# Two PSUM places for the branch products, joined transposes, a final norm in halves, and ten more gates computed early

## The chip, the cores and the metric

The kernel runs on one core of a Trainium2 chip. A core has five engines that work from queues of their own: PE (matrix products), DVE and POOL (elementwise work), ACT (functions and copies) and SP (here only the issuing of transfers). The metric is the device time of one execution in microseconds (us); for the kernel before, three runs gave 1998.32, 1999.73 and 2000.26, median 1999.73.

## The reference

Two layers, each a pre-norm residual layer with three token mixers side by side, on 512 tokens of 1024 channels, all in float32:

```python
def hybrid_layer(x, ...):
    h = rms_norm(x, norm_w)
    p = h @ w_in                        # 1024 x 13440
    xa, ga, pb, pc, pm = jnp.split(p, [OFF_GA, OFF_B, OFF_C, OFF_M], axis=-1)
    y_a = rglru_branch(xa, ...) * silu(ga)     # convolution, gates, scan over tokens
    y_b = rwkv7_branch(pb, ...)                # 16 heads of 64, a state per head updated token by token
    y_c = retention_branch(pc)                 # 4 heads of 256, causal scores with decay
    proj = jnp.einsum("nbsw,nwd->bsnd", ys, w_branch)   # 3 x (1024 x 1024)
    gates = sigmoid(pm + b_merge)              # 3 x 1024 gate channels
    merged = sum over branches of gates * proj
    return x + merged @ w_out
# after two layers: rms_norm(x, final_norm_w)
```

## The kernel before

Everything is kept transposed: channels on the 128 partitions, the 512 tokens along the free axis. A projection (`proj`, line 566) turns one 128-channel block of weights into one 128x512 result: the weight block is loaded (`raw`), split into a rounded part and a remainder (`whi` by ACT, `wlo` by DVE; `weights`, line 557), and eight channel tiles of the input, split the same way, give 24 matmuls into one PSUM tile called `acc`. A layer has 129 such projections: inputs of the three mixers, 24 merge gates (`gate`, line 1109), 24 branch products (`branch`, line 1123: eight for each of the branches b0, b1, b2) and eight output products.

The mixer of the RWKV branch works on two 128-channel blocks at a time, a "head group" (four per layer). For each it has a preparation (`p`), scores (`s`), a chain of eight steps over the token chunks (`c`, `rwkv_chain`) and an output part (`o`). In a chain step PE works three times for a moment (tile `p`), and in between ACT and DVE copy its results (`zs`, `sv`). The scores hold an inversion on POOL (`ex`, `etmp`, 62 operations). Three kinds of small products, `vt`, `w` (its second half) and `yt`, are written in the code once for each of the two blocks of the group.

Nothing is issued in the order of the code. A planner (`Scheduler`, line 156) records every operation, gives each tile slot out in the order of the program, and lists the operations by a cost table and due times; the engines' queues then hold that order, and each engine works through its own. The order of the program comes from the list `ORDER` (line 68): `l` is a part of the recurrent branch, `r` one of the retention branch, `g2` computes the four gates 8 to 11 early and stores them in DRAM (`gsc`), `b0 b2 b1` are the branches at the end of a layer. A gate that was not stored is computed in `branch` right ahead of its product. In PSUM the projections have three places called "a" and one called "d"; a branch product always takes "d", and the next branch product can start once DVE has read it (`stt`, tile `thm`, and for b0 tile `mg`). Slots of SBUF tiles are given by `caps` (line 376): `raw` is a weight block as it was loaded.

All transfers go through SP's queue in order. The final norm (`sum_sq`, `rms_scale` and a loop at the end) sums the squares of the eight tiles `xr`, and multiplies each by its gain and by `rs` on DVE (two of the eight on POOL).

The matrix products of the small kind (`p`, `vt`, `w`, `yt`, `sc`, `lora`) use parts of the array ("tiled"), the projections all of it.

All engine instructions are recorded by one line, 368, so the profile's rows are told apart by the names of tiles: `yh`, `yq` and `ylo` are the inputs of branch products, `mq` that of the output products, `xh` and `xl` those of the first projections of a layer, `hh` and `hl` those of all the others.

Of the kernel before, what the change touches and what calls it, by code (L numbers as in the profile page):

```python
# [13 lines left out]
ACTF = mybir.ActivationFunctionType  # L14
# [3 lines left out]
P = 128  # L18
# [48 lines left out]

ORDER = "p0 l1 s0 l0 g2 p1 c0 l2 o0 s1 p2 g1 l3 c1 r0 o1 s2 r1 p3 c2 r2 o2 s3 r3 c3 o3 b0 b2 b1".split()

# [303 lines left out]
def hybrid_kernel(ctx: ExitStack, tc: tile.TileContext, xT, wt, par, cst, outT):  # L373
    nc = tc.nc
    S = Scheduler(nc)
    caps = {"h": 16, "tp": 16, "tc": 7, "tm": 14, "q": 12, "sv": 1, "raw": 3, "whi": 2, "wlo": 2,
            "zs": 2, "sn": 2, "pc": 2, "ssq": 2, "vm": 2, "vv": 2}
# [187 lines left out]

    def proj(l, w, movs, bank="a", wts=None):
        hi, lo = wts or weights(l, w)
        ps = tl(bank, "acc")
        with S.prio(4):
            for k0 in range(0, KT, 2):  # L570
                with S.group():
                    for k in (k0, k0 + 1):
                        whi, wlo = hi[:, k * P:(k + 1) * P], lo[:, k * P:(k + 1) * P]
                        mh, ml = movs[k]
                        mm(ps[:], whi, mh, k == 0, False, T)
                        mm(ps[:], whi, ml, False, False, T)
                        mm(ps[:], wlo, mh, False, k == KT - 1, T)
        return ps


    def sum_sq(xs, last=None):
        acc = []
        for k in range(KT):
            sq = tl("tm", "sq")
            act(sq[:], xs[k], ACTF.Square)
            if k < 2 or k == KT - 1:
                acc.append(sq)
            else:
                tt(acc[k % 2][:], acc[k % 2][:], sq[:], ALU.add)
            if last:  # L590
                last(k)

# [270 lines left out]
    def rwkv_scores(l, prep, g):  # L863
# [83 lines left out]
        sv = tl("sv", "sv", [P, NCH, 2, 2, HK])  # L947
        for i in range(2):
            ps = tl("rp", "vt", [P, NCH, HK])
            with S.group():  # L950
                for c in range(NCH):
                    for q in range(2):
                        mm(ps[half(q), c, :], v[i][:, c * CH:(c + 1) * CH], blkc[:, half(1 - q)], True, True, HK,
                           tiled="t")
            for q in range(2):
                act(sv[half(q), :, i, 1 - q, :], ps[half(q)], ACTF.Copy)

# [31 lines left out]
        for q in range(2):  # L989
            rr = slice(HK * q + 32, HK * q + 64)  # L990
            act(xw[rr, :, 0:256], ps[rr].rearrange("p i c t -> p i (c t)"), ACTF.Copy)
        for i in range(2):
            ps = tl("rp", "w2", [P, NCH, 32])
            with S.group():
                for c in range(NCH):
                    for q in range(2):
                        mm(ps[half(q), c, :], xw[:, i, 32 * c:32 * c + HK],
                           XD[i][:, c, HK * q + 32:HK * q + 64], True, True, 32, tiled="t")
            for q in range(2):
                rr = slice(HK * q, HK * q + 32)  # L1000
                act(XD[i][rr, :, HK * q + 32:HK * q + 64], ps[rr], ACTF.Copy, scale=-1.0)
        for s_ in range(2):
# [54 lines left out]
    def rwkv_out(l, h, sco, g):  # L1057
# [12 lines left out]
        with S.prio(1):  # L1070
# [7 lines left out]
            act(ssq[:], ssq[:], ACTF.Exp, scale=-0.5)  # L1078
            for i, j in enumerate(js):
                yn = yns[i]  # L1080
                tt(yn, XD[i][:, :, 0:HK], ssq[:, i, :].unsqueeze(2).to_broadcast([P, NCH, HK]), ALU.mult)
                ps = tl("rp", "yt", [P, NCH, CH])
                with S.group():
                    for c in range(NCH):
                        for q in range(2):
                            mm(ps[half(q), c, :], sco[1][i][:, c, 0, :], ident[:, half(1 - q)], True, True, CH, tiled="t")
                y = bonus[i]
# [35 lines left out]
    def branch(l, h, mg, b, where, first, last, stored):  # L1123
        ys = load_y(l, b, where)
        ms = []
        for m in range(KT):
# [6 lines left out]
            if first:  # L1133
                mg.append(tl("tm", "mg"))
            ps = proj(l, W_BR + 8 * b + m, ys, "d")
            with S.prio(0.6):
# [17 lines left out]
    for l in range(DEPTH):  # L1154
        with S.prio(1):
            xw = gained(l, xs)
            ps = sum_sq(xs)
        qs = [tl("tm", "q") for _ in range(4)]
# [41 lines left out]
        def do(kind, n):  # L1200
# [12 lines left out]
            elif kind == "g":  # L1213
                ns = range(4 * n, 4 * n + 4)
                gates(l, h, ns)
# [5 lines left out]
        for x in ORDER:  # L1221
            do(x[0], int(x[1]))
        xs = []
        xq = []
        with S.prio(3):
            for k in range(0, KT, 2):
                t = tl("q", "xr", [P, 2, T])
                for i in range(2):
                    dma(t[:, i], xT[k + i] if l == 0 else xsc[k + i], TILE_B)
                    xs.append(t[:, i])  # L1230
        for m in range(KT):
            ps = proj(l, W_OUT + m, ms, "ad"[m % 2])
            with S.prio(1):
                tt(xs[m], xs[m], ps[:], ALU.add)
    with S.prio(0):
        gain = [pcol(0, "final_norm_w", k) for k in range(KT)]
        ps = sum_sq(xs, lambda k: k % 4 == 1 and act(xs[k], xs[k], ACTF.Identity, scale=gain[k]))
        rs = rms_scale(ps)
        for k in range(KT):
            if k % 4 == 1:  # L1240
                ptt(xs[k], xs[k], rs[:], ALU.mult)
            else:
                stt(xs[k], xs[k], gain[k], rs[:], ALU.mult, ALU.mult)
            dma(outT[k], xs[k], TILE_B)

# [78 lines left out]
```

## Time and profile before

| what | value |
|---|---|
| median of three runs | 1999.73 us |
| the profiled execution | 1998.77 us |
| its span, first to last instruction | 1996.9 us |
| PE busy | 1955.3 us |
| DVE, ACT, POOL busy | 1276.2, 893.7, 571.4 us |
| granted clock of PE, mean | 0.997 |
| transfers | 206.59 MB, mean 103 GB/s |
| weight blocks loaded | 281 of 512 KB, 3.3 us from issue to landing (median) |

The span is 1.87 us shorter than the execution's own time, and that execution is 0.96 us below the median of the runs. Matmuls are pipelined: each shows as busy for about 0.39 us, though the next one starts 0.227 us after it. A busy share of 98% therefore hides short delays, and starts of rows are the better measure. "Idle before" is time in which an engine did nothing ahead of an instruction, with the instruction that ended the wait.

### The profile page before, as it was taken

Reading aid. Unit: us, or ns where it says so; the run is one execution under the profiler, and the core shown is the slowest. Engines: PE = TensorE matmul, PEld = TensorE weight load, DVE = VectorE, ACT = ScalarE, POOL = GpSimd, SP = SyncE. Lnnn points to the kernel's source line nnn. Section 1 sums busy time; section 2 is a strip of 40 time slices with the busy share of each in tenths; the row PEclk is TensorE's granted clock in tenths of the full one; section 3 lists DMA queues with packets and bytes.
Section 4 is the critical chain, followed back from the end, with each engine's and each line's share of the span. In section 5 each row is a group of like instructions: output and inputs, shape, how many; then the busy total and the mean of one; then the engine's idle time right before and its main releaser. Section 6 shows DMA issues by size and latency. Waiting matters only on the chain.

```text
span 1996.9 us, 32028 instructions
## 1 busy us (share of the span) xinstructions
PE 1955.3 (98%) x12792; PEld 1537.1 (77%) x12792; DVE 1276.2 (64%) x1885; ACT 893.7 (45%) x1366; POOL 571.4 (29%) x790
## 2 busy tenths in 40 slices
PE   9999999999999999999999999999999999999997
PEld 6778778868877887778878787787788787768785
DVE  8995677678567753444569747785875687443534
ACT  7663735262344343432357546444432634342322
POOL 1137125521812361000012542273326125400000
PEclk9999999999999999999999999999999999999998
DMA  4243133322322343243522432332223123332441
GB/s 171 87 119 117 64 108 101 96 70 80 109 64 90 106 122 123 87 156 95 178 89 87 133 100 75 109 105 76 86 77 111 54 93 109 121 117 95 151 145 63
DMA packets 104069, 206.59 MB, mean 103 GB/s; under 512 B 42608, under 2 KB 43888, under 8 KB 103920
## 3 DMA queue, kind: packets, MB, share of 16 engines
q1 hardware_dynamic: 103920, 204.55, 31.7%
q8 instruction: 101, 1.65, 0.3%
q14 instruction: 48, 0.39, 0.1%
HBM read 179.34 MB, written 25.17 MB: 102 GB/s over the span
## 4 chain that ended last, share of the span: by engine, by line
PE 86%; DVE 6%; POOL 4%; issue 1%; DMA 1%; ACT 1%; DVEq 0%; SPq 0%; ACTq 0%; POOLq 0%
PE acc L368 65%; PE p L368 5%; PE vp L368 4%; POOL etmp L368 2%; PE rout L368 2%; POOL ex L368 2%; PE w L368 2%; PE sc L368 2%; PE rsc L368 2%; PE gate L368 1%; DVE wlo L368 1%; DVE bk L368 1%; PE yt L368 1%; PE kss L368 1%; PE vt L368 1%
## 5 line engine op out<-in xcount | busy, mean ns | idle before, releaser
L368 ACT ACTIVATE whi<-raw 128x1024 fp32r<-128x1024 f32 (+1 forms) x283 | 298.7, 1055 | 734.8 <-PE acc L368 587.4
L368 PE MATMUL acc<-hh,whi 128*128 128x512 f32 x1488 | 609.7, 410 | 0.1
L368 PE MATMUL acc<-hh,wlo 128*128 128x512 f32 x1488 | 582.4, 391 | 2.9 <-DVE wlo L368 2.9
L368 PE MATMUL acc<-hl,whi 128*128 128x512 f32 x1488 | 580.7, 390 | 0.0
L368 DVE TENSOR_TENSOR wlo<-raw,whi 128x1024 fp32r<-128x1024 f32 (+1 forms) x283 | 365.7, 1292 | 214.4 <-ACT whi L368 211.5
L368 PEld LDWEIGHTS acc<-hh,whi 128*128 128x128 f32 x1488 | 279.2, 188 | 70.8 <-issue 6.5
L368 PEld LDWEIGHTS acc<-hh,wlo 128*128 128x128 f32 x1488 | 279.3, 188 | 65.8 <-DVE wlo L368 5.8
L368 PEld LDWEIGHTS acc<-hl,whi 128*128 128x128 f32 x1488 | 279.8, 188 | 55.9 <-issue 3.8
L368 POOL TENSOR_TENSOR etmp<-ex,ea 64x31 f32<-64x31 f32 (+15 forms) x248 | 174.6, 704 | 44.9 <-DMA ea<-ead 26.2
L368 POOL TENSOR_TENSOR ex<-ex,etmp 64x31 f32<-64x31 f32 (+15 forms) x248 | 172.7, 696 | 19.2
L368 POOL TENSOR_TENSOR dec<-sv,pc 64x128 f32<-64x128 f32 x96 | 48.2, 503 | 403.6 <-DVE sv L368 400.2
L368 ACT ACT_TABLE_LOAD x87 | 111.6, 1283 | 2.3 <-PEq L1315 0.7
L368 PE MATMUL acc<-yh,whi 128*128 128x512 f32 x256 | 104.1, 407 | 8.2 <-DVE thm L368 5.0
L368 PE MATMUL acc<-yh,wlo 128*128 128x512 f32 x256 | 100.2, 391 | 0.0
L368 PE MATMUL acc<-ylo,whi 128*128 128x512 f32 x256 | 99.9, 390 | 0.0
L368 POOL TENSOR_TENSOR bk<-k,pi 64x512 f32<-64x512 f32 x32 | 52.7, 1646 | 151.1 <-DVE k L368 136.3
L368 POOL TENSOR_TENSOR hl<-hf,hh 128x512 fp32r<-128x512 f32 x8 | 15.7, 1978 | 257.7 <-ACT hh L368 257.7
L368 PE MATMUL acc<-yq,whi 128*128 128x512 f32 x256 | 80.0, 394 | 4.3 <-DVE thm L368 4.3
L368 PE MATMUL acc<-mq,whi 128*128 128x512 f32 x256 | 79.3, 391 | 0.0
L368 DVE SCALAR_TENSOR_TENSOR thm<-thm,acc 128x512 f32<-128x512 f32 x32 | 22.0, 687 | 85.8 <-PE acc L368 85.6
L368 PE MATMUL vp<-whi,hh 128*128 128x256 f32 x256 | 75.7, 296 | 0.0
L368 PE MATMUL vp<-wlo,hh 128*128 128x256 f32 x256 | 72.4, 283 | 0.0
(228 smaller groups left out, 3207.8 us busy)
## 6 DMA issues: line engine op xcount, KB each, us to landing
raw<-in_w SPq DMA_DIRECT2D x281, 512.0 KB, 3.3
yl<-ys SPq DMA_DIRECT2D x48, 256.0 KB, 4.1
ys<-thg SPq DMA_DIRECT2D x16, 256.0 KB, 2.2
gs<-thm SPq DMA_DIRECT2D x16, 256.0 KB, 2.2
ys<-bonus SPq DMA_DIRECT2D x16, 256.0 KB, 2.1
ys<-yr SPq DMA_DIRECT2D x16, 256.0 KB, 2.0
thm<-gs SPq DMA_DIRECT2D x16, 256.0 KB, 3.9
x<-in_x SPq DMA_DIRECT2D x8, 256.0 KB, 4.5
```

The lines of the kernel that those rows point to most:

```text
L368: fn(*[r(v) for v in pos], **{k: r(v) for k, v in kw.items()})
```

## The change

The list `ORDER` is rewritten: `gN` now stands for two gates (2N and 2N+1), and nine such parts (gates 4 to 15 and 18 to 23) stand ahead of the branches, where two parts of four (4 to 11) stood before. So 18 of 24 gates of a layer are computed early and go through DRAM; 0 to 3, 16 and 17 are still computed in the branches. A branch product takes PSUM place "d" and one of "a" in turn. The `vt`, `w` and `yt` products of a head group's two blocks form one unit each for the planner. The sum of squares of the first layer is added up on POOL. SBUF slots change: `tc` 7 to 6, `tm` 14 to 16, `raw` 3 to 2. The last output product and the final norm behind it are done for 256 tokens at a time.

```diff
-ORDER = "p0 l1 s0 l0 g2 p1 c0 l2 o0 s1 p2 g1 l3 c1 r0 o1 s2 r1 p3 c2 r2 o2 s3 r3 c3 o3 b0 b2 b1".split()
+ORDER = "p0 l1 s0 g5 l0 g7 p1 g6 c0 l2 o0 g4 s1 p2 g2 g3 c1 o1 l3 s2 r0 r1 p3 g11 c2 r2 g10 o2 s3 r3 c3 g9 o3 b0 b2 b1".split()
...
-    caps = {"h": 16, "tp": 16, "tc": 7, "tm": 14, "q": 12, "sv": 1, "raw": 3, "whi": 2, "wlo": 2,
+    caps = {"h": 16, "tp": 16, "tc": 6, "tm": 16, "q": 12, "sv": 1, "raw": 2, "whi": 2, "wlo": 2,
...
-                tt(acc[k % 2][:], acc[k % 2][:], sq[:], ALU.add)
...
+                add(acc[k % 2][:], acc[k % 2][:], sq[:], ALU.add)
...
-        for i in range(2):
-            ps = tl("rp", "vt", [P, NCH, HK])
-            with S.group():
+        pss = [tl("rp", "vt", [P, NCH, HK]) for _ in range(2)]
+        with S.group():
+            for i in range(2):
                 for c in range(NCH):
...
-            ps = proj(l, W_BR + 8 * b + m, ys, "d")
+            ps = proj(l, W_BR + 8 * b + m, ys, "da"[m % 2])
...
-            ps = sum_sq(xs)
+            ps = sum_sq(xs, ptt if l == 0 else tt)
...
-                ns = range(4 * n, 4 * n + 4)
+                ns = range(2 * n, 2 * n + 2)
...
+        for hf in range(2):
+            cols = slice(256 * hf, 256 * hf + 256)
+            ps = proj(l, None, ms, "ad"[hf], wts=wts, cols=cols)
+            tt(xs[k][:, cols], xs[k][:, cols], ps[:, cols], ALU.add)
+            act(sq[:, cols], xs[k][:, cols], ACTF.Square)
+            act(warm[:], sq[:, 256 * hf:256 * hf + 1], ACTF.Ln, scale=0.0, bias=bcol[:, 0:1])
+            ps = tl("rp", "ss")
+            for n, a in enumerate(acc):
+                mm(ps[:, cols], ones, a[:, cols], n == 0, n == 2, 256)
+            act(rs[:, cols], ps[:, cols], ACTF.Ln, scale=1.0 / D, bias=bcol[:, 0:1])
+            act(rs[:, cols], rs[:, cols], ACTF.Exp, scale=-0.5)
+            for i in range(KT):
+                if i % 4 == 1:
+                    if hf == 0:
+                        act(xs[i], xs[i], ACTF.Identity, scale=gain[i])
+                    ptt(xs[i][:, cols], xs[i][:, cols], rs[:, cols], ALU.mult)
+                else:
+                    stt(xs[i][:, cols], xs[i][:, cols], gain[i], rs[:, cols], ALU.mult, ALU.mult)
+                dma(outT[i][:, cols], xs[i][:, cols], TILE_B // 2)
```

Where the instructions stand now is seen in the queues. First PE at the start of the program, where the first projection of layer 0 (`acc` from `xh`, `xl`) meets the three products that sum the squares over the partitions (`ss`). Before:

```order
L368 MATMUL acc<-xh,whi 128x512
L368 MATMUL acc<-xl,whi 128x512
L368 MATMUL acc<-xh,wlo 128x512
L368 MATMUL ss<-sq,cs 128x512 x3
L368 MATMUL acc<-xh,whi 128x512
L368 MATMUL acc<-xl,whi 128x512
L368 MATMUL acc<-xh,wlo 128x512
```

In the difference of the two queues, at the same place:

```order
 L368 MATMUL acc<-xl,whi 128x512 [waits DVE_49]
 L368 MATMUL acc<-xh,wlo 128x512
-L368 MATMUL ss<-sq,cs 128x512 [waits DMAHW3_49,DVE_49]
-L368 MATMUL ss<-sq,cs 128x512 [waits DVE_49]
+L368 MATMUL acc<-xh,whi 128x512 [waits Activation_49]
+L368 MATMUL acc<-xl,whi 128x512 [waits DVE_49]
+L368 MATMUL acc<-xh,wlo 128x512
+L368 MATMUL acc<-xh,whi 128x512 [waits Activation_49]
+L368 MATMUL acc<-xl,whi 128x512 [waits DVE_49]
+L368 MATMUL acc<-xh,wlo 128x512
+L368 MATMUL ss<-sq,cs 128x512 [waits DMAHW4_49,Pool_49]
```

The six last matmuls of the first projection have moved ahead of `ss`, and `ss` waits for POOL where it waited for DVE.

Next DVE at the end of the program: the additions of the output product (`xr` from `acc`) and the multiplications by gain and `rs`. Before:

```order
L368 TENSOR_TENSOR sq<-sq 128x512
L368 TENSOR_TENSOR xr<-xr,acc 128x512
L368 TENSOR_TENSOR sq<-sq 128x512
L368 TENSOR_TENSOR xr<-xr,acc 128x512
L368 SCALAR_TENSOR_TENSOR xr<-xr,par_139,rs 128x512 x6
```

Now:

```order
L368 TENSOR_TENSOR sq<-sq 128x512
L368 TENSOR_TENSOR xr<-xr,acc 128x256
L368 SCALAR_TENSOR_TENSOR xr<-xr,par_139,rs 128x256 x5
L368 TENSOR_TENSOR xr<-xr,acc 128x256
L368 SCALAR_TENSOR_TENSOR xr<-xr,par_139,rs 128x256 x7
```

The addition of the second token half stands behind five multiplications of the first half.

Last SP's queue at the end of layer 1, from the loads of b1's inputs (`yl`) to those of the residual (`xr`); `raw` are weight blocks, `thm` stored gates. Before:

```order
L368 DMA yl<-ys_11300 128x512 x8
L368 DMA raw<-in_w 128x1024
L368 DMA thm<-gs_9872 128x512 x3
L368 DMA raw<-in_w 128x1024
L368 DMA thm<-gs_9872 128x512
L368 DMA raw<-in_w 128x1024 x11
L368 DMA xr<-xsc 128x512 x5
```

Now:

```order
L368 DMA yl<-ys_11366 128x512 x3
L368 DMA thm<-gs_9587 128x512
L368 DMA raw<-in_w 128x1024
L368 DMA thm<-gs_9587 128x512 x5
L368 DMA raw<-in_w 128x1024
L368 DMA thm<-gs_9587 128x512
L368 DMA raw<-in_w 128x1024
L368 DMA thm<-gs_9587 128x512
L368 DMA raw<-in_w 128x1024 x8
L368 DMA xr<-xsc 128x512 x4
```

All eight gates of b1 now come by transfers between the weight blocks; before, four did, and the other four cost a weight block and a projection each.

## Rows read from the trace of the kernel before

**Rows 1.** The page: busy time, share of the span and instructions.
```profile
PE 1955.3 (98%) x12792; PEld 1537.1 (77%) x12792; DVE 1276.2 (64%) x1885; ACT 893.7 (45%) x1366; POOL 571.4 (29%) x790
```
**Rows 2.** Waits of PE: waiter, releaser, total us, times, longest.
```profile
PE acc L368 <- DVE thm L368: 9.3, 8, 2.1
PE p L368 <- DVE zs L368: 5.8, 8, 1.2
```
**Rows 3.** Groups by shape: count, busy us, mean ns, idle before and releasers.
```profile
L368 PE MATMUL acc<-yh,whi 128*128 128x512 f32 x256 | 104.1, 407 | 8.2 <-DVE thm L368 5.0 <-ACT whi L368 1.7 <-DVE mg L368 1.5
L368 PE MATMUL acc<-yq,whi 128*128 128x512 f32 x256 | 80.0, 394 | 4.3 <-DVE thm L368 4.3
```
**Rows 4.** Timeline, start of b1 in layer 0: start us, us, instruction.
```profile
882.54 0.39 PE L368 MATMUL acc<-yq,wlo 128*128 128x512 f32 x1
882.97 0.69 DVE L368 SCALAR_TENSOR_TENSOR thm<-thm,acc 128x512 f32<-128x512 f32 x1 [1.28 <-PE acc L368]
...
883.80 0.47 PE L368 MATMUL acc<-yh,whi 128*128 128x512 f32 x1 [0.87 <-ACT whi L368]
```
**Rows 5.** The chain that ended last, two undisturbed stretches: start, us, what.
```profile
453.77 4.31 PE vp L368 x36
...
1887.06 90.05 PE acc L368 x396
```
**Rows 6.** Timeline of PE around small tiled products.
```profile
141.27 0.39 PE L368 MATMUL acc<-hh,wlo 128*128 128x512 f32 x1
141.59 1.15 PE L368 MATMUL vt<-cs,v 128*64 128x64 f32 x32
142.67 0.50 PE L368 MATMUL acc<-hh,whi 128*128 128x512 f32 x1
143.01 0.39 PE L368 MATMUL acc<-hl,whi 128*128 128x512 f32 x1
...
501.12 2.08 PE L368 MATMUL vt<-cs,v 128*64 128x64 f32 x64
```
**Rows 7.** The chain that ended last, end of the program.
```profile
1978.83 2.77 PE acc L368 x12
...
1981.63 0.70 DVE xr L368
...
1983.00 1.28 ACT L368
...
1985.18 1.28 ACT L368
...
1987.13 0.75 DVE xr L368
...
1989.55 3.65 DVE xr L368 x4
```
**Rows 8.** Tile xr from 1940 us on: durations min/median/max in ns.
```profile
L368 DVE SCALAR_TENSOR_TENSOR xr<-xr,par,rs x6: 734/744/1752, 1987.1 to 1992.5; 128x512 f32<-128x512 f32 x6
...
L368 POOL TENSOR_TENSOR xr<-xr,rs x2: 1706/1740/1775, 1987.2 to 1989.0; 128x512 f32<-128x512 f32 x2
```
**Rows 9.** Timeline, the first 42 us.
```profile
8.04 0.61 ACT L368 ACTIVATE sq<-x 128x512 f32<-128x512 f32 x1
...
14.93 2.84 PE L368 MATMUL ss<-sq,cs 128*128 128x512 f32 x6
...
38.94 0.41 DVE L368 TENSOR_TENSOR lwl<-lraw,lwh 128x256 fp32r<-128x256 f32 x1
...
41.14 0.50 PE L368 MATMUL acc<-hh,wlo 128*128 128x512 f32 x1 [0.86 <-DVE wlo L368]
```
**Rows 10.** Tile raw: from issue to landing.
```profile
DMA to landing us min/median/max: 3.1/3.3/7.1
```
**Rows 11.** Timeline of PE in a chain step, retention scores between.
```profile
582.59 0.40 PE L368 MATMUL p<-sv,br 128*64 128x64 f32 x8
...
583.98 0.34 PE L368 MATMUL p<-sv,se 128*64 128x64 f32 x4
```

## What I predict, and how

> **What bounds the kernel now.** I read the page first: PE is busy for 1955.3 of 1996.9 us, no other engine above 64% [rows 1]. So the kernel gets faster by what PE stops waiting for, by what PE no longer does, or at the two ends, where PE has nothing to do. I then looked at PE's waits. The largest is for DVE's reading of a branch product (`thm`): 9.3 us in 8 waits; the next is in the chain steps, 5.8 us in 8 [rows 2]. The groups by shape put all waits of branch products on two rows, 8.2 us and 4.3 us, 12.5 us in all [rows 3]. Because matmuls overlap, a busy share hides part of every wait, so I read starts. In undisturbed stretches PE starts a 512-column matmul every 90.05 / 396 = 0.227 us, and a 256-column one every 4.31 / 36 = 0.120 us [rows 5]; a projection of 24 takes 5.45 us. Last I read the two ends of the program, in the chain that ended last and in the timeline [rows 7, 9].
>
> **The change, part by part.**
>
> Branch products in two places. The wait has one form: the last matmul of a product starts at 882.54, DVE reads the tile from 882.97 for 0.69 us, and the next product starts at 883.80 [rows 4]. (The row names ACT's `whi` as the releaser; that split ends at the same moment, but belongs to the product after.) From start to start this is 1.26 us instead of 0.227, so it costs 1.03, while the row shows 0.87 of idle time. With a second place the next product can start at once, and DVE has 5.45 us for its reading. There are five long waits of this kind in a layer, so the 12.5 us of idle time are about 12.5 + 10 x 0.16 = 14.1 us of PE time. The cover is that splitting, gates and loads keep up when products follow each other without a gate's projection between: per 5.45 us DVE then has a split of 1.2 us and up to three operations of 0.7 us, which is below 3.4 us. I take -14.1, and as the other end 0 (below).
>
> Joined transposes. A visit of PE to tiled products costs time at entry and exit. From the start of the last full matmul before a visit with 32 rows of `vt` to the second one behind it is 143.01 - 141.27 = 1.74 us; less two steps of 0.227 that leaves 1.29. A visit with 64 rows is busy 2.08 us, one with 32 1.15, so 32 rows are 0.93, and a visit's fixed cost is 0.35 us [rows 6]. The code now joins three kinds of products, which would be 24 visits saved. But in the queue of before the two halves of `w` and `yt` stood together already in all eight head groups, and those of `vt` in six of eight. Counting all kinds, PE's queue has 260 visits before and 254 now. So 6 x 0.35 = -2.1 us, not the 8.4 that the code suggests. The joined unit waits for both blocks, which costs nothing where they stood together anyway.
>
> Eighteen early gates. The sum of PE's projections is the same, they only move, so the value is 0. What they touch: twenty more stores and loads of 256 KB on SP's queue, in front of weight blocks; and the stretch at the end of a layer, where seven products of b2 and eight of b1 now follow each other, 30 in both layers. A weight block had three slots and has two. A load is issued when the block two before it has been split, so it has two product times less one split; even if that split took a whole product's time 5.4 us would be left, against 3.3 to landing typically and 7.1 at most [rows 10]. And one more split block stands ready in `whi` and `wlo`. I take 0; the bounds are below.
>
> Chains. Around the chains the planner has filled differently: retention products stand between the visits more often. Counted in the queues, the fills without any projection matmul are 8 in a layer before and 15 now. Such a fill is short, but the trace shows one that sufficed: from the visit at 582.59 to the next at 583.98, with 256-column score products between, PE never stopped [rows 11]. The longest wait of a chain is 1.2 us [rows 2]. So 14 more short fills cost between 0 and 14 x 1.2 = 16.8 us; and the 5.8 us of chain waits could go, since more fill is there around. I take 0, nearest to the row that shows such a fill.
>
> Start. The five additions of squares go from DVE to POOL. A POOL multiplication of the same size takes 1.74 us (median), and each of the two in the trace held up one DVE operation by 1.75 - 0.74 = 1.0 us [rows 8]. POOL cannot begin before the third square, at 8.65 [rows 9]; five additions in a row end at 8.65 + 8.7 = 17.4, while `ss` began at 14.93 and is busy for 2.8 [rows 9]. PE now does the six last matmuls of the first projection before `ss`. Before, `ss` and these six were done at 14.93 + 2.8 + 1.4 = 19.1; now at the earliest at 17.4 + 2.8 = 20.2, 1.1 us late. DVE saves 5 x 0.7 and loses 5 x 1.0 in the stretch in which it feeds the first projection, 1.5 us more; with one more held operation PE is up to 1.1 + 1.5 + 1.0 = 3.6 late. Of this the later wait of 0.86 us for `wlo` at 41.14 [rows 9] comes back. Range 0 to +3.6, value +2.5.
>
> A rule speaks against this edit. The Trainium skill (SBUF — State Buffer, "Who interferes with whom") says that a DVE instruction with two inputs in SBUF and a POOL instruction that reads SBUF exclude each other, one being blocked for the whole of the other. In [rows 8] the POOL operation held DVE for 1.0 of its 1.74 us; held in full, five of them would cost the start another 5 x 0.74 = 3.7 us.
>
> End. Last product of the program in halves: 48 matmuls at 0.120 for 24 at 0.227, +0.3 us. Then the norm. Before, from the addition at 1981.63 to the end there are 15.3 us: addition 0.70, square 0.63, table load 1.28, a small Ln, Ln, table load 1.28, Exp, then six multiplications on DVE until 1993.20, and 3.7 us for the last transfer and the end [rows 7]. Counted from the start of the last product (24 matmuls and `ss` between, 7.2 us) this is 22.5. In halves an operation of 256 columns costs 0.41 where one of 512 costs 0.70 [rows 7, 9]. First half: product 2.9, then 5.0 to its `rs`, of which 2.6 are the two table loads, which don't shrink. Then DVE's queue counts: five multiplications of the first half, 5 x 0.41 and two held by POOL for 0.5, stand in front of the second half's addition. That addition could run at 8.1 (its product is done after 2.9 + 2.2 of `ss` + 2.9) and runs at 11.0. From there 4.6 to the second `rs`, 3.5 for six multiplications, 3.6 to the end: 22.7. So the halves pay for two more table loads and a queue in the wrong order: +0.2, range -2.8 (if the addition were not held) to +1.
>
> The Trainium skill (ScalarE: Activation LUTs, "What ACT_TABLE_LOAD costs") gives about 2.66 us for a switch of table, with a drain. In this trace the load is 1.28 us and `rs` is ready 1.95 us after it began, Exp included [rows 7]; by the page the end would lose another 2 x 1.4 us, an estimate.
>
> Sum: -14.1 - 2.1 + 0 + 0 + 2.5 + 0.3 + 0.2 = -13.2 us on the profiled execution's 1998.77, so 1985.6. The median of the runs was 0.96 above that execution: 1986.5 us.
>
> **The rivals.**
>
> More gain: the start loses nothing and the chain waits go: 1986.5 - 2.5 - 5 = 1979. For it: more fill in every stretch. Against: the waits in chains come from DVE being late, not from missing fill.
>
> Held in full: POOL's additions block DVE for all of their time at the start, +3.7, so 1990. For it: both in [rows 8] overlapped DVE at once. Against: the 1.0 us measured there. (This is the rule of SBUF — State Buffer in the Trainium skill.)
>
> Chains wait: if the 14 added short fills each wait half of 1.2 us, +8.4, 1995; if all wait in full, 2003. For it: DVE works for retention at that time too. Against: [rows 11].
>
> Slower than before: the products without gates between starve. Place: the 30 products in a row at the ends of the layers, with two weight slots and the gates' loads in the same queue. Each such product that comes late waits for a split; from 13.2 / 30 = 0.44 us a product the gain is gone, at 1.0 us the time is 1986.5 + 30 = 2016. For it: 768 KB per 5.45 us, where a gate's projection used to double the time. Against: landing in 3.3 us with 5.4 or more to go.
>
> No effect: the change doesn't do what it says, as the three "a" places are given in program order and a product must wait for a gate that holds one. Then the 14.1 stay and 1999 to 2001 results. Against: only six gates of a layer are left there.
>
> **How the numbers follow.** Forecast 0.62 (its own range 1981 to 1992), more gain 0.10, held in full 0.06, chains wait 0.10, starving 0.07, no effect 0.05. A difference of 0.2%, 4 us, is about what a measurement of this kernel tells from none. Faster are the first three and a third of the chains' case, 0.81; within 0.2% are the rest of the chains' case and most of no effect, 0.11; slower 0.08. The range 1979 to 1999 leaves out the starving case and the ends of two others.
>
> **What would show it.** In the profile after: the waits of branch products for `thm` fall from 12.5 us to under 2; `vt` has 64 rows in every visit, `w` and `yt` as before; the first `hh` projections start 2 to 3 us later than before; between the last product's start and the end still about 22 us; chain waits near 6 us. I would be wrong if PE waits for `wlo` or for `thm` loads in the 30 products, if waits in the chains of the second and third head group grow by several us, or if the start loses more than 4.

## The result and the profile after

The changed kernel takes 1973.87 us (median of four runs, 1973.38 to 1974.98) against 1999.99 for the kernel before beside it: ratio 0.9872, interval 0.9855 to 0.9889. So it is faster by 26.1 us, twice the 13.2 us forecast, and below the range. The span fell from 1996.9 to 1971.6 us.

The first line of the page after, to be held against [rows 1] (busy time, share, instructions):

```profile
PE 1947.8 (99%) x12822; PEld 1544.9 (78%) x12822; DVE 1262.5 (64%) x1887; ACT 914.1 (46%) x1384; POOL 574.4 (29%) x797
```

PE's idle time is 1971.6 - 1947.8 = 23.8 us where it was 41.6. PE's waits after (waiter, releaser, total us, times, longest), all that the view lists:

```profile
PE acc L368 <- DVE xl L368: 4.7, 4, 2.1
PE ss L368 <- ACT sq L368: 3.5, 1, 3.5
PE p L368 <- DVE zs L368: 2.2, 2, 1.1
PE idle L368 <- DVE warm L368: 1.5, 1, 1.5
PE acc L368 <- DVE wlo L368: 1.3, 2, 0.7
```

The waits for `thm` of [rows 2] are gone, and those of the chains fell from 5.8 to 2.2 us. `xl` and `ss` are the two ends of the program. The groups by shape that answer to [rows 3] (busy us, mean ns, idle before):

```profile
L368 PE MATMUL acc<-yh,whi 128*128 128x512 f32 x256 | 104.1, 407 | 0.0
L368 PE MATMUL acc<-yq,whi 128*128 128x512 f32 x256 | 78.8, 389 | 0.0
```

12.5 us of idle time became 0. All of PE's visits to `vt` now have 64 rows, as here in the timeline (start us, us), where [rows 6] had one with 32:

```profile
141.13 2.08 PE L368 MATMUL vt<-cs,v 128*64 128x64 f32 x64
```

At the start the row that stood at 41.14 in [rows 9] is later, in the timeline of PE:

```profile
45.35 0.50 PE L368 MATMUL acc<-hh,wlo 128*128 128x512 f32 x1 [0.69 <-DVE wlo L368]
```

That is 4.2 us. At the end, DVE's timeline (compare [rows 7]):

```profile
1956.99 3.00 DVE L368 SCALAR_TENSOR_TENSOR xr<-xr,par,rs 128x256 f32<-128x256 f32 x5 [4.18 <-ACT rs L368]
1959.92 0.41 DVE L368 TENSOR_TENSOR xr<-xr,acc 128x256 f32<-128x256 f32 x1
1960.25 0.47 DVE L368 SCALAR_TENSOR_TENSOR xr<-xr,par,rs 128x256 f32<-128x256 f32 x1
1964.50 3.50 DVE L368 SCALAR_TENSOR_TENSOR xr<-xr,par,rs 128x256 f32<-128x256 f32 x6 [3.78 <-ACT rs L368]
```

The addition of the second half (1959.92) stands behind five multiplications, although PE had begun the last matmul of its product at 1957.09:

```profile
1957.09 0.28 PE L368 MATMUL acc<-mq,wlo 128*128 128x256 f32 x1
```

Where nothing stands in front of it (e8 below) the addition begins 0.32 us after that matmul does, so here it was held for about 2.5 us. This is the queue in the wrong order that the prediction described.

So the parts that were foreseen are there, and still 13 us more went. By the starts of PE's rows in the kernel before, ten branch products begin directly behind another and are 12.7 us late in all; six that stand among the last chains add 1.9. None of these 14.6 us is left. The rest came from many small waits in the mixers: the last steps of chains, the gates of the recurrent branch, the retention scores. Where the chain waits came from can be read in the kernel before. DVE, POOL and ACT, then PE, around one of them, in the second head group's chain; the first number is the start, the second the duration:

```profile
442.30 1.83 POOL L368 TENSOR_TENSOR bk<-k,pi 64x512 f32<-64x512 f32 x1
442.90 1.77 DVE L368 TENSOR_TENSOR ra<-ra,rb 128x512 f32<-128x512 f32 x1
443.73 0.27 ACT L368 ACTIVATE zs<-p 64x128 f32<-64x128 f32 x1 [3.54 <-PE p L368]
444.60 0.68 DVE L368 TENSOR_TENSOR rc<-rc,rd 128x512 f32<-128x512 f32 x1
445.31 0.29 DVE L368 COPY zs<-p 64x128 f32<-64x128 f32 x1
...
622.94 2.99 POOL L368 TENSOR_TENSOR bk<-k,pi 64x512 f32<-64x512 f32 x2
623.25 3.23 DVE L368 TENSOR_TENSOR bk<-ksq,pi 64x512 f32<-64x512 f32 x2
626.51 0.29 DVE L368 COPY zs<-p 64x128 f32<-64x128 f32 x1
626.86 0.45 PE L368 MATMUL p<-zs,xd 128*64 128x64 f32 x8 [1.00 <-DVE zs L368]
```

ACT's half of `zs` is copied at 443.73, DVE's at 445.31. DVE was in `ra`, which took 1.77 us where its neighbour `rc`, of the same shape, took 0.68, because POOL worked on scores (`bk`) beside it; in the third group two `bk` of DVE take 3.23 us. The chain step then waits for a copy of 0.29 us.

### The profile page after: what moved, and what is told of

Read it like the earlier page. It is cut to its first block, busy times and chain, and to the rows that moved or that the text cites. A ratio compares the mean times of both kernels' runs of the same rounds, so it can differ in the third digit from the quotient of the medians.

```text
span 1971.6 us, 32177 instructions
## 1 busy us (share of the span) xinstructions
PE 1947.8 (99%) x12822; PEld 1544.9 (78%) x12822; DVE 1262.5 (64%) x1887; ACT 914.1 (46%) x1384; POOL 574.4 (29%) x797
## 4 chain that ended last, share of the span: by engine, by line
PE 95%; DVE 3%; issue 0%; ACT 0%; DMA 0%; SPq 0%; DVEq 0%; ACTq 0%
PE acc L368 71%; PE p L368 5%; PE vp L368 5%; PE gate L368 2%; PE rsc L368 2%; PE sc L368 2%; PE rout L368 2%; PE w L368 2%; PE yt L368 1%; PE vt L368 1%; PE lora L368 1%; PE tr L368 1%; PE bps L368 1%; PE kss L368 1%; DVE wlo L368 0%
## 5 line engine op out<-in xcount | busy, mean ns | idle before, releaser
L368 DVE TENSOR_TENSOR wlo<-raw,whi 128x1024 fp32r<-128x1024 f32 (+1 forms) x283 | 358.3, 1266 | 186.7 <-ACT whi L368 183.4
L368 POOL TENSOR_TENSOR etmp<-ex,ea 64x31 f32<-64x31 f32 (+15 forms) x248 | 170.2, 686 | 44.6 <-DMA ea<-ead 25.8
L368 POOL TENSOR_TENSOR ex<-ex,etmp 64x31 f32<-64x31 f32 (+15 forms) x248 | 168.8, 681 | 19.4
L368 PE MATMUL acc<-mq,whi 128*128 128x512 f32 (+1 forms) x272 | 79.9, 377 | 0.0
L368 DVE TENSOR_SCALAR sv<-p 64x128 f32<-64x128 f32 x64 | 18.8, 295 | 90.7 <-ACT sv L368 71.9
L368 PE MATMUL vp<-whi,hl 128*128 128x256 f32 x256 | 72.3, 282 | 0.0
```

The lines of the kernel that those rows point to most:

```text
L368: fn(*[r(v) for v in pos], **{k: r(v) for k, v in kw.items()})
```

## The experiments

The theory after the comparison: the new ORDER moved such operations away from the ends of chains, or gave PE enough other work to cover them; the POOL sum costs more than forecast. Rivals: the second place alone, the slots, the joined transposes. Each time is a median, and each ratio is against the kernel before on the same chip. The medians of the kernel before that belong to them run from 1999.8 to 2001.2 us, so between kernels of different tables a difference of one or two us isn't told from none.

**Places alone, places with order, the sum on DVE, eight gates.**

```
e1: before, with   ps = proj(l, W_BR + 8 * b + m, ys, "da"[m % 2])
e2: as e1, with the new ORDER (18 gates); nothing else
e3: after, with    ps = sum_sq(xs, tt)
e4: after, with ORDER less g7 g6 g11 g10 g9 (8 gates early)
```

> The kernel before with one edit: a branch product takes PSUM place d and one of a in turn. Theory (the second place takes away the branch products' waits and nothing else): the starts of PE's rows put 15.9 us on these waits, so 1999.99 - 15.9 = 1984 us, no branch product waits for thm any more, and the waits in the chains (5.8 us by the profile) stay. Rival 1 (the second place is worth all of it, since products that don't wait also end every later wait): 1974, like the changed kernel. Rival 2 (the place that is taken from the other projections makes those wait): 1990 or more.

> The kernel before with two edits: the two PSUM places and the new ORDER with its 18 early gates; slots, start, end and the unjoined transposes stay as before. Theory (the new order moves the ends of the chains, the recurrent gates and the retention scores away from the operations that made DVE late, some 11 us of waits that the prediction had put at 0): 1984 - 11 = 1973, with chain waits under 3 us. Rival 1 (the slots of raw, tm and tc, or the joined transposes, did that): 1984, the same as with the places alone. Rival 2 (three weight slots and more loads in the queue collide): over 1984.

> The changed kernel with the first sum of squares back on DVE. Theory (POOL's additions are late themselves and hold DVE up while it feeds the first projection): the first projections of hh start 4.4 us earlier, 1973.9 - 4.4 = 1969.5. Rival (the six matmuls that were moved ahead of ss make the start late, not POOL): 1973 to 1974.

> The changed kernel with only 8 of its 18 early gates (those of g5, g4, g2, g3), all parts in the new order otherwise. Theory (it is the arrangement of the parts that frees the chains, not the number of gates): 1974 to 1976, chain waits near 2 us. Rival (the ten more gates give PE something to do around the chains and the recurrent and retention products): these waits come back, 11 us, so 1983 to 1986.

| kernel | us | ratio to before (interval) |
|---|---|---|
| e1 places alone | 1986.84 | 0.9930 (0.9915 to 0.9945) |
| e2 places and order | 1971.43 | 0.9852 (0.9836 to 0.9869) |
| e3 sum on DVE | 1968.77 | 0.9840 (0.9825 to 0.9854) |
| e4 eight gates | 2014.21 | 1.0066 (1.0051 to 1.0081) |

The places give 14.3 us, close to the 14.1 of the prediction (the expectation of e1 said 15.9), and the order another 15.4 on top, where 11 were expected. The waits of e1, then those of e2:

```profile
PE p L368 <- DVE zs L368: 5.8, 8, 1.2
PE acc L368 <- DVE wlo L368: 5.4, 9, 0.8
```

```profile
PE p L368 <- DVE zs L368: 2.8, 4, 0.9
...
PE acc L368 <- DVE wlo L368: 1.8, 3, 0.9
```

In e1 the waits for `zs` are untouched, 1.9 us of waits for ACT's `sv` are new, and waits for `wlo` grew from 2.9 to 5.4 us; with the order all of these fall. The sum on DVE is worth 5.1 us by the medians, and 4.3 by the row that the changed kernel has at 45.35 (41.01 in e3). And e4 fell on the far side of both expectations: the new arrangement with eight gates is slower than the kernel before. Its timeline of PE, in the last chain of layer 0:

```profile
808.75 0.45 PE L368 MATMUL p<-zs,xd 128*64 128x64 f32 x8 [0.76 <-DVE zs L368]
810.04 0.45 PE L368 MATMUL p<-sv,tb 128*64 128x64 f32 x8 [0.83 <-DVE sv L368]
810.32 0.56 PE L368 MATMUL p<-sv,br 128*64 128x64 f32 x8
811.29 0.48 PE L368 MATMUL p<-sv,se 128*64 128x64 f32 x4 [0.41 <-DVE sv L368]
...
813.16 0.70 PE L368 MATMUL p<-zs,xd 128*64 128x64 f32 x8 [0.75 <-DVE zs L368]
814.69 0.70 PE L368 MATMUL p<-sv,tb 128*64 128x64 f32 x8 [0.83 <-DVE sv L368]
```

No projection stands between the steps, so PE waits at each for the copies of ACT and DVE. And the clock falls (stretch; busy us of PE, PEld, DVE, ACT, POOL; granted clock; DMA share; GB/s):

```profile
804.00:808.00 4.00, 3.23 (x46) 2.27 (x46) 2.10 (x4) 1.62 (x3) 0.80 (x2) 1.00 0.21 56
808.00:810.00 2.00, 0.45 (x8) 0.31 (x8) 0.59 (x2) 0.54 (x2) 0.00 (x0) 1.00 0.42 158
810.00:812.00 2.00, 1.55 (x30) 1.40 (x32) 0.58 (x2) 1.04 (x4) 0.79 (x2) 0.60 0.00 0
812.00:814.00 2.00, 1.11 (x16) 0.73 (x13) 0.29 (x1) 0.34 (x3) 0.00 (x0) 0.50 0.00 0
...
818.00:820.00 2.00, 2.00 (x6) 1.61 (x5) 1.30 (x3) 0.36 (x2) 0.00 (x0) 0.50 0.00 0
```

Between about 810 and 820 us PE runs at the lower of its levels, 1.2 GHz, after it had been busy for 0.45 of 2 us. So e4 loses in two ways, by waits and by the clock. About 34 us of e4 ran at the lower level (around 274, 810, 1264 and 1800 us), and at half the clock that is up to 17 us, an estimate, of the 40 by which it lies above the changed kernel.

**Joins, old arrangement, two repairs, copies on ACT.**

```
e5: after, with vt, w, yt recorded block by block as before
e7: after, with ORDER = "p0 l1 s0 g5 l0 g7 p1 g6 c0 l2 o0 g4 s1 p2
    g2 g3 l3 c1 r0 o1 s2 r1 p3 g11 c2 r2 g10 o2 s3 r3 c3 g9 o3 b0 b2 b1"
e8: e3, and at the end
+        S.behind = added        # the second half's addition
         ...stt(xs[i][:, cols], xs[i][:, cols], gain[i], rs[:, cols], ...)
e9: before, with   act(zs[half(1)], p1[half(1), cc, :, 1, :], ACTF.Copy)
```

In e8 the planner must put the final multiplications behind that addition (the two gains on ACT are recorded ahead of it); only DVE's queue differs from that of e3.

> The changed kernel with vt, w and yt recorded once for each of the two blocks, as before. Theory of the prediction (joining saves six visits at 0.35 us): 1973.9 + 2.1 = 1976. Rival (the new order alone brings the halves together; PE's queue has 252 visits without the joins against 254 with them): 1973 to 1974.

> The changed kernel with the parts in the order of before, and all 18 early gates put in between them. Theory after the run with 8 gates (it is the number of early gates that matters, since their projections are work without conditions for PE beside the chains): 1974 to 1978, chain waits under 4 us. Rival (number and arrangement are needed together): 1983 or more, with chain waits as before.

> The changed kernel with two repairs: the first sum of squares on DVE (measured: 1968.8), and at the end the addition of the second token half ahead of the multiplications of the first on DVE. Theory of the prediction (the addition waits 2.8 us behind them, and the end hangs on it): 1968.8 - 2.8 = 1966.0. Rival (the last multiplications and transfers set the end, whatever comes first): 1968.8.

> The kernel before with one edit: both copies zs of a chain step on ACT, none on DVE. Theory (PE waits in the chains because DVE's copy stands behind a score operation that POOL stretches): the 5.8 us of waits for zs fall under 2 us, 2000 - 4 = 1996. Rival 1 (the waits are in the chain itself, not in DVE's queue): they stay, 2000. Rival 2 (two copies in a row on ACT make each of 64 steps 0.3 us longer where fill is short): over 2002.

| kernel | us | ratio to before (interval) |
|---|---|---|
| e5 not joined | 1975.23 | 0.9878 (0.9865 to 0.9892) |
| e7 old arrangement, 18 gates | 1974.03 | 0.9870 (0.9857 to 0.9884) |
| e8 both repairs | 1966.55 | 0.9831 (0.9818 to 0.9845) |
| e9 copies on ACT | 2023.85 | 1.0116 (1.0102 to 1.0130) |

e7 equals the changed kernel: with 18 gates the arrangement of the parts carries nothing. e5 is 1.4 us slower, which the intervals don't tell from none. It has 252 visits in its queue against 254, so the joins save no visits here; what does differ is the waits for `zs`, 4.5 us instead of 2.2. e8 is the best version, 33.3 us below the kernel before. Its addition now comes when its product is done (DVE's timeline):

```profile
1953.23 0.42 DVE L368 TENSOR_TENSOR xr<-xr,acc 128x256 f32<-128x256 f32 x1 [4.60 <-PE acc L368]
1953.56 3.01 DVE L368 SCALAR_TENSOR_TENSOR xr<-xr,par,rs 128x256 f32<-128x256 f32 x6
1957.83 3.49 DVE L368 SCALAR_TENSOR_TENSOR xr<-xr,par,rs 128x256 f32<-128x256 f32 x6 [1.25 <-ACT rs L368]
```

That was worth 2.2 us by the medians and 1.9 by the spans (1966.8 and 1964.9 us), of 2.8 forecast. e9 is no test: the planner, given other costs, laid out all queues anew, and the new plan has long waits of its own, 11.2 us for `thm` and 9.1 for `sv` among them.

**Copies on ACT with the order kept; all but the order; slots; the order alone.**

```
e10: before, with the copy planned for DVE and issued on ACT
+    S.rec("DVE", lambda out, in_: nc.scalar.activation(out=out, in_=in_, func=ACTF.Copy),
+          0.15 + zs[half(1)].size / 960.0, dict(out=zs[half(1)], in_=...))
e11: after, with the ORDER of before (8 gates; g2 written as g4 g5, g1 as g2 g3)
e6: after, with the slots of before
e17: before, with the new ORDER; all branch products in place d
```

> The kernel before; DVE's half of every copy zs is issued on ACT, at the place in the order that the planner had given it for DVE, so that all queues but these two stay as they were. Theory (PE's chain waits come from DVE's queue, where a score operation that POOL stretches stands ahead of the copy): the 5.8 us of waits for zs go to under 1.5 us, total 2000 - 4 = 1996. Rival 1 (two copies in a row on ACT make the chain late everywhere): the waits move to ACT zs and the time stays or grows, 2000 to 2004.

> The changed kernel with the ORDER of before, so with 8 early gates; two places, joins, slots, start and end as in the changed kernel. With the run of 18 gates in the old order of the parts (1974.0) it shows what ten more early gates are worth. Theory (number of gates): 1986 to 1990, that is the places alone plus 5 for the start less some for the end. Rival (slots and joins carry part of the gain): 1980 or less. Rival (fill runs out at the end of the mixers, as with the new order and 8 gates): over 2000.

> The changed kernel with the SBUF slots of before (raw 3, tm 14, tc 7). Theory (the slots are not what the gain comes from): 1972 to 1975. Rival (the two more tm slots are needed for stored gates and branch inputs): 1980 or more.

> The kernel before with the new ORDER alone; every branch product still takes place d. Theory (a product right behind a product waits 1.03 us for DVE's reading, and 15 instead of 5 in a layer now stand so): against the run with order and places (1971.4) 30 x 1.03 = 31 us more, 2002. Rival (the order is worth its 15 us without the second place): 1985.

| kernel | us | ratio to before (interval) |
|---|---|---|
| e10 copies on ACT, same order | 1994.78 | 0.9973 (0.9963 to 0.9983) |
| e11 all but the order | 2004.13 | 1.0019 (1.0009 to 1.0028) |
| e6 old slots | 1974.08 | 0.9869 (0.9856 to 0.9883) |
| e17 order alone | 2005.93 | 1.0028 (1.0016 to 1.0039) |

e10 settles the chain waits. PE's queue is that of the kernel before, the waits for `zs` are gone from the list, and for 5.8 us of them 5.5 us came back (3.4 to 7.4 by the interval). Of this the chains' own share is nearer 5: its list has 0.9 us more for ACT's `sv`, and 1.2 us less for the retention scores (`rsc` behind `pt`). What is left of `p` in it:

```profile
PE p L368 <- ACT sv L368: 0.9, 2, 0.5
```

With 18 gates the slots carry nothing (e6). The order without the second place (e17, on record as e2_order_only) costs 34.5 us against e2, whose PE queue is the same. In e17 28 products begin directly behind another, each 1.26 us from start to start where a step is 0.23, so 1.03 us late: 28.9 us in all, and the rest in smaller waits. Its two groups of branch products by shape:

```profile
L368 PE MATMUL acc<-yh,whi 128*128 128x512 f32 x256 | 105.5, 412 | 15.3 <-DVE thm L368 10.5 <-ACT whi L368 3.5 <-DVE mg L368 1.3
L368 PE MATMUL acc<-yq,whi 128*128 128x512 f32 x256 | 80.1, 394 | 10.4 <-ACT whi L368 8.7 <-DVE thm L368 1.7
```

So places and order need each other. And e11 is the surprise: all edits but the order are 4 us slower than before. In the old arrangement eight gates take 2004.1 us and 18 (e7) 1974.0, in the new one 2014.2 (e4) and 1973.9: it is the number of early gates that matters. Only e4 and the changed kernel differ by ten gates alone; between e11 and e7 four others (8 to 11) are moved too. And what ten gates are worth depends on what is around them: 15.4 us from e1 to e2, 30.1 from e11 to e7, 40.3 from e4 to the changed kernel.

**What makes eight gates slow.**

```
e12: e8, with e10's edit
e13: after, with ORDER less g10 g9 (14 gates)
e14: e11, not joined (as e5)      e15: e11, with the slots of before
e16: e8, with ORDER "... c3 g9 g8 o3 g0 g1 b0 b2 b1" (24 gates)
```

> The version with both repairs (1966.5), and DVE's half of every copy zs issued on ACT at the same place of the order. Theory (what is left of the chain waits comes from DVE's queue too): its 2.2 us of waits for zs go, 1964.5 or a little less. Rival (with 18 gates early, two copies in a row on ACT cost as much in other steps): 1966 to 1968.

> The changed kernel with 14 of its 18 early gates (without g9 and g10, which stand late in the order). Theory (the gates are a supply of work without conditions; time is lost only where it runs out, and with eight it ran out in the last chain, at 798 to 816 us): 14 are enough or nearly, 1974 to 1980. Rival (every early gate is worth the same, (2014 - 1974) / 10 = 4 us): 1990.

> The kernel with all edits but ORDER (2004.1), and vt, w and yt recorded block by block again. Question: why these edits lose 17 us against the places alone (1986.8), of which 5 are the start. Theory (the joined units come later or earlier in the plan, and the last chain has no fill left): without the joins the last chain's waits go, 1990 to 1993. Rival (the slots): 2004.

> The kernel with all edits but ORDER (2004.1), and the SBUF slots of before. Theory (the 16 slots of tm instead of 14, or the two of raw instead of three, let the first branch's products run ahead of the last chain, which then has no fill): 1990 to 1993. Rival (the joins do it): 2004.

> The version with both repairs (1966.5) and all 24 gates early: g8 right behind g9, g0 and g1 behind o3. Theory (the supply no longer runs out with 18; more of it changes nothing but the transfers): 1965 to 1968. Rival (every further gate takes waits away, 1.3 us each as from 14 to 18): 1959. Rival (24 products in a row wait for splits or for stored gates): 1972 or more.

Beside the times stands a count from the traces: the projections (24 `acc` matmuls each) that PE starts between the first and the last `p` of the last head group's chain. It is the same in both layers. Between the first `zs` product of that chain and its last `p` there are 22 gaps between PE's visits, and projections are queued in pieces of six matmuls, so 5.5 projections would fill each gap once.

| kernel | gates early | projections in the last chain | us |
|---|---|---|---|
| e8; after; e7 | 18 | 7.0 | 1966.55; 1973.87; 1974.03 |
| e1 | 8 | 6.5 | 1986.84 |
| before | 8 | 6.25 | 1999.99 |
| e13 | 14 | 6.25 | 1978.98 (0.9896, 0.9881 to 0.9911) |
| e16 | 24 | 6.0 | 1986.22 (0.9933, 0.9917 to 0.9950) |
| e9 | 8 | 5.25 | 2023.85 |
| e14 | 8 | 5.0 | 2002.41 (1.0012, 1.0002 to 1.0021) |
| e4 | 8 | 4.25 | 2014.21 |
| e15 | 8 | 4.25 | 2022.60 (1.0110, 1.0095 to 1.0125) |
| e11 | 8 | 4.0 | 2004.13 |

Of these, all kernels with 5.25 projections or fewer are slower than the kernel before, and none with 6 or more. (The other kernels with 18 gates have 6.75 to 7.25; e17, with 7.0, is slow by its branch products.) The gaps without any projection tell the same: none in the kernel before and in those with 18 gates, one in e1 and e13, two in e9 and e16, four in e14, seven in e4, e11 and e15. In e11 7.25 branch products of the layer had been done before the last chain began (4.25 in the kernel before, 2.0 in the changed one), so few were left to stand between its steps. e14 and e15 missed their expectations of 1990 to 1993: neither the joins nor the slots by themselves use the supply up, and e15, with the old slots, is 18 us slower than e11. With eight gates the plan sits close to the edge, and re-planning after an edit can push it over; which edit does, these runs don't settle. The count isn't all either: e9, e14 and e15 also have waits elsewhere, and where gaps are empty the clock takes its part, with a mean of 0.987 in e4, 0.990 in e15 and 0.991 in e11, against 0.995 to 0.998 in every kernel with 14 or 18 gates. e13's theory held: 14 gates lose 5 us, not 16.

With 24 gates there is a new wait (e16's list, then its timeline of SP's queue, ACT and PE):

```profile
PE p L368 <- DVE zs L368: 5.9, 4, 1.9
PE acc L368 <- ACT yq L368: 5.6, 2, 2.8
```

```profile
851.66 3.92 SPq L368 DMA_DIRECT2D yl<-ys  x8
...
856.03 2.56 ACT L368 ACTIVATE yq<-yl 128x512 fp32r<-128x512 f32 x4 [1.24 <-DMA yl<-ys]
...
856.71 0.50 PE L368 MATMUL acc<-yq,whi 128*128 128x512 f32 x1 [2.79 <-ACT yq L368]
```

b0 without any gate of its own is over before the inputs of b2 are loaded and split. That is 5.6 of some 20 us that e16 lies above e8. The first steps of the last chain wait too (`zs`), and between 780 and 800 us the granted clock was 0.91; the rest stays open. Of the numbers tried, 18 is the best.

e12 missed: 1968.24 (0.9842, 0.9827 to 0.9856). The 2 us that it was to gain over e8 didn't come; whether the 1.7 us above e8 are a loss, the intervals don't tell. Its waits:

```profile
PE p L368 <- ACT zs L1020: 2.6, 4, 1.0
...
PE p L368 <- ACT sv L368: 1.7, 2, 0.8
```

In this order ACT is the engine that comes late: which of the two should copy depends on what stands around it.

## Why the prediction was right, and where it wasn't

The direction was right, and so was the largest term of its sum: the branch products, -14.1 forecast, -14.3 in e1. e1's interval (11.0 to 17.0 us) can't tell the reading by starts from the 12.5 us of idle time; e17 can, with 1.03 us a product as the prediction read it. Its "five long waits of this kind in a layer" are four: of the ten in both layers two have another form, DVE coming late itself, and cost 2.3 us each. As the sum went by the idle time of all of them, it came out near. In the row of 30 products it priced every one, and 28 begin behind another. The cover that it named (a split and three operations in 5.45 us) held: no wait for `thm` is left.

The step that failed is "Eighteen early gates. The sum of PE's projections is the same, they only move, so the value is 0", and with it "Chains ... I take 0". With two places in both, the order with its ten more early gates is worth 15.4 us (e2 against e1). That it is their number that counts is shown by e4 against the changed kernel, which differ by the ten gates alone, and by e7. That projections that only move are worth nothing holds while PE never lacks one; but they are what PE does while DVE is late. Where the 15.4 us went is shown in part. From e1's list of waits to e2's 9.0 us are gone (20.3 to 11.3): `zs` from 5.8 to 2.8, `wlo` from 5.4 to 1.8, the retention scores' 0.9 and the recurrent gates' 0.8 to nothing. The other 6 us stand in no list, and their cause is open. That the chain waits are DVE's lateness is shown by e10, for about 5 us in the order of before. The waits of the recurrent gates, `wlo` and the retention scores had been in the views and weren't priced at all. `wlo` and the scores waited for DVE, the recurrent gates for ACT (`thg`); why these were late wasn't tested.

The rival "more gain" had the right mechanism at 5 us and a chance of 0.10, and the argument against it ("DVE being late, not missing fill") sets apart two things that belong together: fill hides lateness. Of the signs, chain waits near 6 us were expected and 2.2 came.

The rival "chains wait" and the starving of 30 products both failed. Starving did exist, elsewhere: not in the products behind the gates, but in the last chain, and the change moved away from it.

The start was mis-sized: +2.5 forecast within 0 to +3.6, and 4.2 to 5.1 came, by the row and by e3; that the start loses more than 4 was one of the signs of being wrong. The sum of squares on POOL took 8.7 us as worked out. The five operations that were to be held for 1.0 us each, 5.0 in all, were others: two `xl` for 1.0 each, and three tiny ones that the prediction didn't have, for 1.1 each. DVE's queue in the changed kernel:

```profile
10.45 1.24 DVE L368 TENSOR_TENSOR sp<-par,sp 128x8 f32<-128x8 f32 x1
...
12.28 1.25 DVE L368 TENSOR_SCALAR sp<-sp 128x8 f32<-128x8 f32 x1
...
14.70 4.77 DVE L368 SCALAR_TENSOR_TENSOR xl<-x,par,xh 128x512 fp32r<-128x512 f32 x4
```

Of these four `xl` two took 0.74 us each, as without POOL, and the two that were held 1.77 and 1.75. What was missed is that `ss` stood behind six more matmuls whose `xl` came late, and that PE, waiting for them, fell to half its clock, so that its matmuls started 0.42 to 0.43 us apart where 0.23 is a step at full clock (PE's timeline):

```profile
14.83 0.63 PE L368 MATMUL acc<-xh,wlo 128*128 128x512 f32 x1
...
15.25 0.63 PE L368 MATMUL acc<-xh,whi 128*128 128x512 f32 x1
```

From 14 to 20 us the granted clock was 0.50, where the kernel before and e3 have 1.00. So `ss` was done at 23.8 us, 6.0 later than before. Half of that is hidden: in the kernel before `rs` wasn't waiting for `ss`, but stood behind a table load of ACT until 20.8. It began 3.0 us late, and the projections that need it 4.2. The later wait for `wlo`, which the prediction counted back, stayed (0.69 for 0.86 us).

The joins: six visits fewer, as counted, but the runs put the reduction down to the order: e2's plan without joins has 252 visits, e1's 258. What the joins themselves save is not clear of noise (1.4 us in e5).

The end was right in its mechanism and nearly in its size: 19.4 us from the first half's product to the end against 19.8 worked out, and 22.3 from the last product's start against about 22. The queue in the wrong order cost 2.2 by e8, 2.8 forecast. Slots 0: right with 18 gates (e6).

Summed up: places -14.3, order -15.4, start +5.1, joins, slots and end together -2.7 (e3 against e2), -27.3 in all. These are the steps of one row of kernels, so their sum has to close and confirms nothing; the 26.1 at the top differs from it only by the two medians of the kernel before (1999.99 and 2001.15).

## What to carry to other kernels

Work without conditions, here projections whose inputs have long been there, is what hides the latency of dependent chains; so count how much of it stands in each chain, the last one above all, before you price a move of it at nothing. Where a planner lays out everything anew after each edit, test a mechanism with the order kept (as e10 did, where e9 told nothing), and expect that two edits that look independent are worth more, or less, together. A result place that is read by another engine wants a twin as soon as two products can follow each other.

## What the runs showed of the hardware

A DVE operation of 128x512 with two inputs in SBUF that starts while POOL works on SBUF tiles mostly gets through only when POOL has ended: in the kernel before 57 of 63 TENSOR_TENSOR of this kind, typically 0.55 us after POOL. In the first 20 us of the changed kernel two of POOL's additions end at 15.93 and 17.60 us, and the `xl` beside them, 0.74 us long by themselves, at 16.48 and 18.15, 0.55 later in both; so does `ra` in the rows of the kernel before (444.67 after 444.13). A tiny operation of the changed kernel is held as well, and ends with POOL's:

```profile
616.39 1.63 POOL L368 TENSOR_TENSOR so<-r,pp 64x512 f32<-64x512 f32 x1
616.87 1.18 DVE L368 TENSOR_SCALAR se<-ksq 64x8 f32<-64x8 f32 x1
```

Not every operation is held. The copy of `zs` at 445.31 in the rows above, which reads PSUM, took its 0.29 us while a POOL operation went on (445.21 to 446.48).

So what a POOL operation costs a DVE operation that it holds isn't a share of its time, as the prediction had it with 1.0 of 1.74 us; it is nearly what is left of it when DVE's operation begins. The Trainium skill (SBUF — State Buffer, "Who interferes with whom") says that the pair of ports that DVE and POOL share is an exclusive lock, and that a DVE instruction with two inputs in SBUF contends for it with a POOL instruction that reads SBUF. These rows agree. POOL is held too: an addition that began 0.02 us after an `xl` (13.44) took 2.47 us, over that `xl` and the `wlo` behind it (to 14.78), where one took 1.28 at 10.39.

In e4, when the last chain ran out of projections, PE's clock fell to its lower level for about 10 us (the rows above), so that the first matmuls behind the chain were slow as well: 1.05 us for two of `yq` at 818.38, 0.62 at 822.80. At the start of the changed kernel, with PE waiting for `xl`, it fell in the same way.
